# More steps of seven products in a stick-breaking attention trunk, with gated heads spilled as ready halves

## Chip, cores and metric

The kernel runs on one core of one Trainium2 chip. The metric is the device time of one execution, in microseconds (us), and the number given for a kernel is the median of its runs. Engines are named as the profile names them: PE is TensorE (PEld its weight loads), DVE is VectorE, ACT is ScalarE, POOL is GpSimd, SP is SyncE.

## The reference

One layer of attention on x (256 rows of 4096), float32 throughout, and a final norm:

```python
xn = rms_norm(x, norm_attn)                     # (256, 4096)
q, k, v, g = split(xn @ w_in_attn, 4)           # w_in: 4096 x 16384; 32 heads of 128
z = q @ k.T / sqrt(128)                         # per head, 256 x 256
a = sigmoid(z) * prod_{s<j<t}(1 - sigmoid(z_tj))  # s < t, worked out in logs
o = a @ v
h = x + (o * silu(g)) @ w_out_attn              # w_out: 4096 x 4096
out = rms_norm(h, final_norm)
```

The convolution's inputs are not used, since the depth is 1.

## The kernel before

**Splitting.** PE multiplies in a format with a shorter mantissa, so each float32 operand is split in two: ACT copies it into that format (`wh`, `nh`, ...; line 172 for weights), DVE subtracts the copy from the full value (`wl`, `nl`; `minus`, line 98). A product is then three matmuls of 128x128 by 128x512: high by high, high by low, low by high (`mm3`, lines 426 to 428).

**Units and steps.** The work is a list of 21 units (lines 101 to 110). Units 0 to 15 read w_in, two for each of eight column groups j: the even one makes q and k of four heads, the odd one g and v. Units 16 to 20 read w_out: 16 to 18 make two column blocks of 512 each, 19 and 20 one each. A unit runs through 16 steps s; a step takes 256 of the 4096 rows of the weights (two chunks of 128, two column blocks: four pieces of 128x512, 1 MB), and multiplies them with the two row blocks of the activations.

**Seven or eight products.** A step of such 2x2 blocks needs eight products (`EIGHT_PARTS`, or "plain" in units 0, 1 and 16). In the steps named in `SEVEN` it makes seven, from sums of blocks (`SEVEN_PARTS`): three more additions on the weights by DVE (lines 160 to 164), and seven weight pieces to split instead of four. The sums on the activations' side (the "forms") are built once, by `build`, and kept split in SBUF for all units: seven forms for a step in `SEVEN`, six for another, four for a plain one. `combine_early` and `combine_late` put a unit's banks together at its end.

**What sets the order.** Everything is written out in one stream, and the build then orders each engine's instructions, which each engine runs in order. Weight pieces are loaded by SP into three buffers `raw`; the halves of a pair of pieces go into one of `PAIRS` = 4 buffers, a single piece into `SINGLES` = 1; `split` (line 152) is called as far ahead as these allow (lines 690 to 697). A buffer comes free when PE has used it. The remaining work is hung on (unit, step) slots by `at` (lines 571 to 664) and is emitted behind that step's products: for each head `heads_T` (transposes of q and k, and their split), `scores`, `weights_of` (the logs, their suffix sums by matmul, and exponentials), `heads_out`; for each group `gate`, `gate_T`, `v_parts`. `rows_out` (line 379) copies the banks of units 0 and 1.

**Gated heads.** `heads_out` leaves o times the gate in a tile `gated`, which POOL writes to HBM (`spill`, line 497). In unit 15 each step's heads are read back and split (`load_heads`, `build_heads`, what "o"), as w_in's forms of that step are done with; in unit 16 they are read again and built into seven or six forms ("p"), the last two at the end of its step 15; in unit 18 the plain forms of the `SEVEN` steps are built once more ("r"), for the units of one column block.

**Rooms.** Tiles of attention share rooms by tag: `v` (5 buffers: v, its halves, and at the start the loads of x), `f` (2), `qkh`, `qkl` and others (1 each). `gh` (2 buffers) holds what `build` reads and the gated heads.

Of the kernel before, what the change touches and what calls it, by code (L numbers as in the profile page):

```python
# [9 lines left out]
F32 = mybir.dt.float32  # L10
# [27 lines left out]
SEVEN = (2, 4, 6, 9, 11, 13)  # L38
# [11 lines left out]
SEVEN_FORMS = ("A11", "A12", "A22", "S1", "S2", "S3", "S4")  # L50
# [20 lines left out]
def kernel(  # L71
# [41 lines left out]
    for u, (kind, w, cols) in enumerate(units):  # L113
        for s in range(NS):
# [5 lines left out]
            else:  # L120
# [6 lines left out]
                else:  # L127
                    which = SEVEN_PARTS if s in SEVEN else EIGHT_PARTS
# [48 lines left out]
    nc.scalar.dma_start(gcol, gain_in)  # L177
# [4 lines left out]
    def load_x(i):  # L182
        if i >= NS:
            return
        xs[i] = ap.tile([P, KT, S], F32, tag="v", name=f"xs{i}", bufs=5)
        for part in ([slice(0, 1), slice(1, 2)] if i == 0 else [slice(0, 2)]):
            nc.sync.dma_start(xs[i][:, part, :], xT[i][:, part, :])
# [25 lines left out]
    def build(i, y, kind, what):  # L213

        names = {"plain": PLAIN_FORMS, "mixed": SEVEN_FORMS if i in SEVEN else EIGHT_FORMS}[kind]
        h, l = new_forms(i, names, what)

# [3 lines left out]

        if names is not SEVEN_FORMS:
            both(slice(0, 4), y)
            if names is EIGHT_FORMS:
                d = room(f"d{what}{i}", 2)
                y4 = y.rearrange("p (a b) c -> p a b c", a=KT)
                nc.vector.tensor_tensor(out=d, in0=y4[:, :, 0, :], in1=y4[:, :, 1, :], op=ALU.subtract)  # L227
                both(slice(4, 6), d)
            return
        d = room(f"d{what}{i}", 4)  # L230
        tt = nc.vector.tensor_tensor
        tt(out=d[:, 0, :], in0=y[:, 1, :], in1=y[:, 3, :], op=ALU.subtract)
        tt(out=d[:, 1, :], in0=d[:, 0, :], in1=y[:, 0, :], op=ALU.subtract)
        tt(out=d[:, 2, :], in0=y[:, 0, :], in1=y[:, 1, :], op=ALU.subtract)
        tt(out=d[:, 3, :], in0=y[:, 2, :], in1=d[:, 1, :], op=ALU.add)
        both(slice(0, 1), y[:, 0:1, :])
        both(slice(1, 3), y[:, 2:4, :])
        both(slice(3, 7), d)

    def room(name, n):  # L240
        pool, tag = (ap, "f") if ep is None else (ep, "junk")
        return pool.tile([P, n, P], F32, tag=tag, name=name, bufs=2 if ep is None else 1)

    def load_y(src, name):
        y = wp.tile([P, 4, P], F32, tag="gh", name=name, bufs=2)
# [5 lines left out]
    def load_xn(i):  # L251
        if i < NS:
            ys[i] = load_y(xT[i], f"xn{i}")
# [494 lines left out]
```

## Time and profile before

| | |
|---|---|
| median of 3 runs | 1807.13 us (1803.22 to 1808.31) |
| the profiled execution | 1806.54 us; span from first to last instruction 1804.6 us |
| granted TensorE clock, mean | 0.996 |
| ACT busy in the pair of units 12 and 13 (177.1 us) | 108.6 us |
| DMA share and rate in that pair | 0.55, 194 GB/s |
| DMA issues of POOL | 16 of xn, 16 of spill, 16 of o, 16 of p, 6 of r, 256 KB each |

The profile is of one execution. A row of a group gives the line, engine and operation, the tile written and those read, the count, then busy us, mean ns of one, and the idle time of its engine just ahead with what ended it. A row of the timeline begins with the start in us and the duration. A row of a stretch gives its ends and length, then busy us and count of PE, PEld, DVE, ACT and POOL, the granted clock, the DMA engines' share and GB/s. A row of the waits gives who waited, for whom, us in total, times, and the longest.

### The profile page before, as it was taken

To read this page: it belongs to the slowest core of one execution; us is meant where nothing else is said; L and a number is where in the kernel's file an instruction comes from. 1 tells how busy PE (TensorE), PEld (TensorE's weight loads), DVE (VectorE), ACT (ScalarE), POOL (GpSimd) and SP (SyncE) were. 2 spreads that over 40 slices of the span, in tenths; PEclk is the share of its full clock that TensorE was granted. 3 is DMA by queue.
4 is the path that set the end of the run, shared out by engine and by line. 5 is a ranking of instruction groups with operands and counts; after the bars stand their busy time and mean duration, and the time that the engine had idled before them with its cause. 6 is when DMAs were issued, how large, how long until landed. Compare 5 with 4: busy or idle time off the path is not lost. (4 is left out here: it accounts for less than half of the span.)

```text
span 1804.6 us, 22433 instructions
## 1 busy us (share of the span) xinstructions
PE 1778.2 (99%) x8107; PEld 1469.9 (81%) x8107; DVE 1495.3 (83%) x1810; ACT 1089.5 (60%) x1449; POOL 39.5 (2%) x80
## 2 busy tenths in 40 slices
PE   8999999999999999999999999999999999999997
PEld 6888788888888888888888888888887888788885
DVE  5678988888888888888888888888888977889854
ACT  5765665666566656665666565656565756655642
POOL 0000000000000000000000000000001011000000
PEclk9999999999999999999999999999999999999999
DMA  8856555555555545555555555555556666656664
GB/s 313 304 197 223 197 182 195 190 193 197 188 205 191 195 177 216 192 194 184 196 202 186 196 196 193 187 192 190 195 194 221 241 231 219 236 220 239 245 228 150
DMA packets 108814, 374.25 MB, mean 207 GB/s; under 512 B 12704, under 2 KB 12960, under 8 KB 108704
## 3 DMA queue, kind: packets, MB, share of 16 engines
q1 hardware_dynamic: 102960, 354.46, 54.8%
q0 software_dynamic: 5600, 18.35, 3.1%
q8 instruction: 63, 1.03, 0.2%
q14 instruction: 47, 0.39, 0.1%
q10 hardware_dynamic: 144, 0.02, 0.0%
HBM read 364.40 MB, written 8.39 MB: 207 GB/s over the span
## 5 line engine op out<-in xcount | busy, mean ns | idle before, releaser
L172 ACT CAST wh<-raw 128x1024 fp32r<-128x1024 f32 (+1 forms) x833 | 818.8, 1001 | 609.7 <-PE acc L428 274.8
L98 DVE TENSOR_TENSOR wl<-raw,wh 128x1024 fp32r<-128x1024 f32 (+1 forms) x833 | 950.6, 1159 | 245.0 <-ACT wh L172 236.5
L426 PE MATMUL acc<-wh,nh 128*128 128x512 f32 x1708 | 672.9, 394 | 2.2 <-ACT v_sb L383 1.9
L427 PE MATMUL acc<-wl,nh 128*128 128x512 f32 x1708 | 666.4, 390 | 2.7 <-DVE wl L98 2.3
L428 PE MATMUL acc<-wh,nl 128*128 128x512 f32 x1708 | 666.3, 390 | 0.0
L427 PEld LDWEIGHTS acc<-wl,nh 128*128 128x128 f32 x1708 | 321.1, 188 | 68.7 <-DVE wl L98 5.6
L428 PEld LDWEIGHTS acc<-wh,nl 128*128 128x128 f32 x1708 | 320.6, 188 | 68.0
L426 PEld LDWEIGHTS acc<-wh,nh 128*128 128x128 f32 x1708 | 320.9, 188 | 66.4 <-ACT v_sb L383 2.3
L426 PE MATMUL acc<-wh,ph 128*128 128x512 f32 x324 | 125.8, 390 | 2.1 <-ACT wh L172 1.5
L427 PE MATMUL acc<-wl,ph 128*128 128x512 f32 x324 | 126.5, 391 | 0.1
L428 PE MATMUL acc<-wh,pl 128*128 128x512 f32 x324 | 126.1, 389 | 0.0
L160 DVE TENSOR_TENSOR raw<-raw 128x1024 f32<-128x1024 f32 x96 | 117.4, 1223 | 2.3
L426 PE MATMUL acc<-wh,sh 128*128 128x512 f32 x256 | 101.3, 396 | 4.4 <-DVE sh L205 4.4
L427 PE MATMUL acc<-wl,sh 128*128 128x512 f32 x256 | 100.9, 394 | 0.7 <-DVE wl L98 0.6
L428 PE MATMUL acc<-wh,sl 128*128 128x512 f32 x256 | 100.4, 393 | 0.0
L426 PEld LDWEIGHTS acc<-wh,ph 128*128 128x128 f32 x324 | 60.7, 188 | 16.2 <-ACT wh L172 2.7
L427 PEld LDWEIGHTS acc<-wl,ph 128*128 128x128 f32 x324 | 60.8, 188 | 14.0 <-DVE wl L98 1.4
L428 PEld LDWEIGHTS acc<-wh,pl 128*128 128x128 f32 x324 | 60.8, 188 | 12.6
L164 DVE TENSOR_TENSOR raw<-raw 128x512 f32<-128x512 f32 x96 | 66.2, 690 | 2.4
L163 DVE TENSOR_TENSOR raw<-raw 128x512 f32<-128x512 f32 x96 | 66.1, 688 | 1.7
L426 PEld LDWEIGHTS acc<-wh,sh 128*128 128x128 f32 x256 | 48.7, 190 | 15.0 <-ACT wh L172 5.1
L427 PEld LDWEIGHTS acc<-wl,sh 128*128 128x128 f32 x256 | 48.8, 191 | 11.5 <-DVE wl L98 1.5
(167 smaller groups left out, 1374.1 us busy)
## 6 DMA issues: line engine op xcount, KB each, us to landing
raw<-in_w_in_dram SPq DMA_DIRECT2D x510, 512.0 KB, 4.2
raw<-in_w_out_dram SPq DMA_DIRECT2D x128, 512.0 KB, 4.2
xn<-in_xT_dram POOLq DMA_DIRECT2D x16, 256.0 KB, 3.0
xr<-in_x_dram SPq DMA_DIRECT2D x16, 256.0 KB, 5.0
spill<-gated POOLq DMA_DIRECT2D x16, 256.0 KB, 4.1
o<-spill POOLq DMA_DIRECT2D x16, 256.0 KB, 3.6
p<-spill POOLq DMA_DIRECT2D x16, 256.0 KB, 3.8
xres<-in_x_dram SPq DMA_DIRECT2D x16, 256.0 KB, 4.3
```

The lines of the kernel that those rows point to most:

```text
L98: nc.vector.tensor_tensor(out=out_, in0=full, in1=part.bitcast(F32), op=ALU.subtract)
L160: nc.vector.tensor_tensor(out=r[:, 0:3:2, :], in0=r[:, 0:4:3, :], in1=r[:, 2:3, :].broadcast_to([P, 2, CW]), op=ALU.add)
L163: nc.vector.tensor_tensor(out=r[:, 3, :], in0=r[:, 0, :], in1=r[:, 3, :], op=ALU.add)
L164: nc.vector.tensor_tensor(out=r[:, 1, :], in0=r[:, 3, :], in1=r[:, 1, :], op=ALU.add)
L172: nc.scalar.copy(wh[n][:, c, :], f)
L426: nc.tensor.matmul(out_, ah, bh, start=start, stop=False, **kw)
L427: nc.tensor.matmul(out_, ah, bl, start=False, stop=False, **kw)
L428: nc.tensor.matmul(out_, al, bh, start=False, stop=stop, **kw)
```

## The change

- `SEVEN` has eight steps instead of six, for the units of w_in; `SEVEN_OUT` (seven steps) is used for those of w_out. Two steps of seven now stand next to each other in places.
- `build` has no plain kind any more, and puts the sums into the tile that it reads; `room` is gone.
- Gated heads are split once, when they are made (`heads_parts`), and three tiles are spilled: full, high half, low half. The plain forms "o" and "r" are then loaded as halves (`load_parts`), with no work on ACT and DVE. "p" is still built from the full tile; step 15's is built from the tile in SBUF, and the builds of steps 14 and 15 stand in steps 0 and 1 of unit 17.
- v has moved from room `v` (now 4 buffers) to `qkh` and `qkl`, as has the scratch of `gate`; `bound` is one copy of 128x128 that is broadcast; the squares' scratch uses `qkl`.
- Slots of `heads_T`, `scores`, `weights_of`, `heads_out` have moved; `v_parts` stands ahead of `gate`.
- The first piece of x and the gain are issued by ACT instead of SP, ahead of the weights; `rows_out` copies bank C22 ahead of C12.

```diff
-SEVEN = (2, 4, 6, 9, 11, 13)
+SEVEN = (2, 3, 5, 7, 8, 10, 12, 13)
+SEVEN_OUT = (2, 3, 5, 7, 10, 12, 13)
...
-                    which = SEVEN_PARTS if s in SEVEN else EIGHT_PARTS
+                    which = SEVEN_PARTS if s in (SEVEN if w is w_in else SEVEN_OUT) else EIGHT_PARTS
...
-    nc.scalar.dma_start(gcol, gain_in)
...
-        xs[i] = ap.tile([P, KT, S], F32, tag="v", name=f"xs{i}", bufs=5)
-        for part in ([slice(0, 1), slice(1, 2)] if i == 0 else [slice(0, 2)]):
-            nc.sync.dma_start(xs[i][:, part, :], xT[i][:, part, :])
+        xs[i] = ap.tile([P, KT, S], F32, tag="v", name=f"xs{i}", bufs=4)
+        if i:
+            nc.sync.dma_start(xs[i], xT[i])
+            return
+        for k in range(KT):
+            nc.scalar.dma_start(xs[i][:, k, :], xT[i][:, k, :])
+            if k == 0:
+                nc.scalar.dma_start(gcol, gain_in)
...
+        tt(out=y[:, 3, :], in0=y[:, 1, :], in1=y[:, 3, :], op=ALU.subtract)
+        tt(out=y[:, 1, :], in0=y[:, 0, :], in1=y[:, 1, :], op=ALU.subtract)
+        tt(out=y[:, 0, :], in0=y[:, 3, :], in1=y[:, 0, :], op=ALU.subtract)
+        tt(out=y[:, 2, :], in0=y[:, 2, :], in1=y[:, 0, :], op=ALU.add)
+        both(slice(3, 7), y)
...
-    for i in range(RAW_BUFS - 1):
-        load(i)
-        load_x(i)
+    load_x(0)
+    load(0)
+    load_x(1)
+    load(1)
     load_x(2)
...
-        st["v", j] = [ap.tile([P, CW], F32, tag="v", name=f"v_sb{j}_{t}", bufs=5) for t in range(NT)]
+        st["v", j] = [ap.tile([P, CW], F32, tag="qk" + "hl"[t], name=f"v_sb{j}_{t}") for t in range(NT)]
...
+        for dst, r, col, t in ((one, r1, 1, 0), (one, r1, 1, 1), (two, r2, 2, 1), (two, r2, 2, 0)):
+            nc.scalar.activation(dst[t], bank[PLAIN[f"C{t + 1}{col}"]], AF.Copy, scale=r[:, t : t + 1])
...
-        if k == KT - 1:
-            spill[s] = dp.tile([P, 4 * P], F32, name=f"spill{s}")
-            nc.gpsimd.dma_start(spill[s], st["o", s].rearrange("p a b -> p (a b)"))
...
+    def heads_parts(s):
+
+        gated = st["o", s]
+        oh = ap.tile([P, 4, P], F32R, tag="qkh", name=f"oh{s}")
+        ol = ap.tile([P, 4, P], F32R, tag="qkl", name=f"ol{s}")
+        nc.scalar.copy(oh, gated)
+        minus(ol, gated, oh)
+        for what, t in (("f", gated), ("h", oh), ("l", ol)):
+            spill[s, what] = dp.tile([P, 4, P], t.dtype, name=f"spill_{what}{s}")
+            nc.gpsimd.dma_start(spill[s, what], t)
+
+    def load_parts(s, what):
+
+        for part, t in zip("hl", new_forms(s, PLAIN_FORMS, what)):
+            nc.gpsimd.dma_start(t, spill[s, part])
...
-        for i, s in ((0, 2), (1, 8)):
+        for i, s in ((0, 5), (1, 10)):
             at(u + 1, s, heads_T, j, i)
             at(u + 1, s + 1, scores, j, i)
             at(u + 1, s + 3, weights_of, j, i)
+        at(u + 2, 0, v_parts, j)
         at(u + 2, 0, gate, j)
-        at(u + 2, 0, v_parts, j)
...
+            ((3, gate_T, j, 0), (4, heads_out, j, 0), (4, heads_out, j, 1), (4, heads_parts, 2 * j), (7, heads_T, j, 2),
+             (8, scores, j, 2), (10, weights_of, j, 2), (11, gate_T, j, 1), (12, heads_out, j, 2), (12, heads_T, j, 3),
+             (13, scores, j, 3), (15, weights_of, j, 3), (17, heads_out, j, 3), (17, heads_parts, 2 * j + 1))
...
+    for s in range(NS):
+        at(*{NS - 2: (U, 4), NS - 1: (U, 13)}.get(s, (U - 1, max(s, 2))), load_parts, s, "o")
+
+    for s in range(NS - 1):
+        for i in ((0, 1) if s == 0 else (s + 1,)):
+            if i < NS - 1:
+                at(U, s, load_heads, i)
+        at(U + s // (NS - 2), s % (NS - 2), build_heads, s)
+    at(U + 1, 1, lambda: build(NS - 1, st["o", NS - 1], SEVEN_OUT, "p"))
...
+    for s in SEVEN_OUT:
+        at(LAST - 2, s, load_parts, s, "r")
```

More of the change, by code (lines that the diff above doesn't have):

```diff
@@ L278 @@
     make_identity(nc, ident)
-    bound = ap.tile([P, 2, P], F32, name="bound")
+    bound = ap.tile([P, 1, P], F32, name="bound")
     nc.gpsimd.memset(bound, 3e38)
@@ L626 @@
     at(U, 15, make_room)
-    for s in (NS - 2, NS - 1):
-        at(U, 15, build_heads, s, "mixed", "p")
     for c in (0, 1):
```

93 lines of the change are left out of this document (28 added, 65 removed).

## The prediction

> **What bounds the kernel now.** I read the page's busy row first, then the waits of PE, then busy time by stretch, and last the timelines of two places. Units are numbered as the kernel's list has them (0 to 15 read w_in, 16 to 20 w_out); I cut the stretches at a unit's first product, found by counting products in PE's timeline. "Step" is one of a unit's sixteen.
>
> ```profile
> span 1804.6 us, 22433 instructions
> PE 1778.2 (99%) x8107; PEld 1469.9 (81%) x8107; DVE 1495.3 (83%) x1810; ACT 1089.5 (60%) x1449; POOL 39.5 (2%) x80
> ...
> PE acc L426 <- DVE sh L205: 4.4, 1, 4.4
> PE acc L427 <- DVE wl L98: 2.9, 3, 1.4
> PE acc L426 <- ACT v_sb L383: 1.9, 1, 1.9
> PE acc L426 <- ACT wh L172: 1.5, 2, 1.3
> ```
>
> TensorE sets the end: its four longest kinds of wait for others sum to 10.7 us in the whole run, and 4.4 of that is the start. A busy PE isn't yet a PE at its pace, so the pace comes from starts. Here is one step of seven products (unit 12, step 2) and the first product behind it:
>
> ```profile
> 1091.67 0.39 PE L426 MATMUL acc<-wh,nh 128*128 128x512 f32 x1
> ...
> 1096.43 0.39 PE L426 MATMUL acc<-wh,nh 128*128 128x512 f32 x1
> ```
>
> 21 matmuls in 4.76 us: 0.227 us each, though a row says 0.39. A step of eight is 24 of them, 5.45 us.
>
> The stretches are units 12, 13, 15, 17 and 18, then 12 and 13 as a pair:
>
> ```profile
> 1080.80:1170.40 89.60, 89.60 (x421) 74.74 (x420) 78.06 (x90) 55.02 (x71) 0.54 (x1) 1.00 0.53 192
> 1170.40:1257.90 87.50, 87.50 (x404) 72.83 (x403) 74.55 (x84) 53.57 (x68) 0.54 (x1) 1.00 0.56 196
> 1347.60:1438.90 91.30, 89.62 (x403) 72.11 (x401) 82.85 (x99) 59.70 (x83) 8.59 (x16) 1.00 0.63 227
> ...
> 1535.00:1622.10 87.10, 84.85 (x368) 68.26 (x367) 74.47 (x82) 51.29 (x64) 0.00 (x0) 1.00 0.63 226
> 1622.10:1705.30 83.20, 83.20 (x368) 68.60 (x367) 75.84 (x85) 49.74 (x62) 3.22 (x6) 1.00 0.67 240
> ...
> 1080.80:1257.90 177.10, 177.10 (x822) 147.57 (x821) 152.61 (x173) 108.59 (x138) 1.08 (x2) 1.00 0.55 194
> ```
>
> Three things to see. In the pair PE has no gap, and VectorE is busy 152.6 of 177.1 us: near, but behind. Unit 15 has unit 13's products and takes 3.8 us longer. Unit 17 has unit 18's and takes 3.9 longer.
>
> **Products removed.** The fourteen mixed w_in units (2 to 15) go from six to eight steps of seven, the two of w_out (17, 18) from six to seven: 14 x 2 + 2 = 30 steps, three matmuls less in each. 90 x 0.227 = **-20.4 us**, 2.7 in each pair of w_in units. The built order agrees: 8017 matmuls for 8107. All of it lies on the engine that sets the end.
>
> **What a step of seven costs VectorE.** These rows are groups by shape, then a stretch of its timeline:
>
> ```profile
> L98 DVE TENSOR_TENSOR wl<-raw,wh 128x1024 fp32r<-128x1024 f32 x735 | 891.4, 1223 | 238.3 <-ACT wh L172 230.0
> L172 ACT CAST wh<-raw 128x1024 fp32r<-128x1024 f32 x735 | 767.6, 1052 | 582.5 <-PE acc L428 274.8 <-DVE raw L160 204.7 <-DVE raw L164 58.3
> ...
> L98 DVE TENSOR_TENSOR wl<-raw,wh 128x512 fp32r<-128x512 f32 x98 | 67.2, 685 | 6.7 <-ACT wh L172 6.5
> L164 DVE TENSOR_TENSOR raw<-raw 128x512 f32<-128x512 f32 x96 | 66.2, 690 | 2.4
> ```
>
> ```profile
> 1082.75 1.22 DVE L98 TENSOR_TENSOR wl<-raw,wh 128x1024 fp32r<-128x1024 f32 x1
> 1083.88 1.29 DVE L394 SCALAR_TENSOR_TENSOR gl<-g_sb,gl 128x512 f32<-128x512 f32 x2
> ...
> 1089.17 0.69 DVE L98 TENSOR_TENSOR vl<-v_sb,vh 128x512 fp32r<-128x512 f32 x1
> 1089.77 0.69 DVE L163 TENSOR_TENSOR raw<-raw 128x512 f32<-128x512 f32 x1
> ...
> 1091.58 0.68 DVE L164 TENSOR_TENSOR raw<-raw 128x512 f32<-128x512 f32 x1
> 1093.43 5.23 DVE L98 TENSOR_TENSOR wl<-raw,wh 128x1024 fp32r<-128x1024 f32 x5 [1.18 <-ACT wh L172]
> 1098.59 1.22 DVE L160 TENSOR_TENSOR raw<-raw 128x1024 f32<-128x1024 f32 x1
> 1099.84 0.69 DVE L163 TENSOR_TENSOR raw<-raw 128x512 f32<-128x512 f32 x1
> ```
>
> A wide instruction lasts 1.22 us but the next, independent one starts 1.13 to 1.14 later; a narrow one 0.60. One that reads the result starts 1.25 later (1098.59 to 1099.84), 0.11 to 0.12 more, which makes 0.72 for a narrow one. A step of eight is two wide splits, 2.28. A step of seven is three wide splits, a narrow one and three additions: 3.42 + 0.60 + 1.25 + 0.72 + 0.61 = 6.6. Four more such steps in a pair add 4 x 4.3 = 17.3, and the split of the gated heads, new there, 2 x 0.60. So 152.6 + 18.5 = 171.1, while PE's pair shrinks to 174.4. On average VectorE still fits, at 98%, and ScalarE easily does. What decides is where the steps stand.
>
> **The new neighbours.** The sets had no two steps of seven in a row; now 2-3, 7-8 and 12-13 are, so 14 x 3 = 42 places in w_in and 2 x 2 = 4 in w_out. The four pair buffers hold the halves ahead of PE. When PE starts the first seven (time 0), the second's first cast can only begin, as PE has just left the step before. From ScalarE's timeline, the lag behind PE and behind an addition:
>
> ```profile
> 1078.32 1.05 ACT L172 CAST wh<-raw 128x1024 fp32r<-128x1024 f32 x1 [0.24 <-PE acc L428]
> ...
> 1092.35 4.43 ACT L172 CAST wh<-raw 128x1024 fp32r<-128x1024 f32 x5 [1.95 <-DVE raw L164]
> ```
>
> The second seven then goes: cast 0.24 to 1.3; on VectorE the first split to 2.4, L160 to 3.6, the narrow split to 4.2, L163 to 4.8, a wide split to 5.9, L164 until 6.6; only then the last cast, 0.1 + 1.05, to 7.8; the last split ends at 9.0 (L160 and L163 are taken at their shorter spacing, as the built order puts other work between). PE wants it at 4.76 + 15 x 0.227 + 0.23 = 8.4. So a place is 0.6 us short before any attention work. A lone seven, as before, has a step of eight ahead of it, in which VectorE needs 2.3 us and PE 5.45, and comes in time. The built order of the changed kernel puts two matmuls that need only the cast in front of that wait (-0.2), and in some places the next step's or the attention's products. Attention work on VectorE between the two makes it worse: the gate in 2-3, scores and splits in 7-8 and 12-13. I followed both orders of one pair of units through with these spacings. The even unit is short by 0.25 at step 3, 1.45 at step 8 (split of the gated heads and gating stand ahead), 0 at 13; the odd one by 0.25, 0.55 and 0.5. That is 3.0 in six places, **0.5 each; 46 x 0.5 = +23.0 us**. Ends: 0 (before's sevens, lone, cost PE nothing in the pair's row) and 1.2 (no reordered product helps, and one more narrow instruction, 0.60, stands in each). I take 0.5, between, since it follows the order that is built.
>
> **The start.** PE's first product waited for VectorE's L205, that for the transfer of xs:
>
> ```profile
> 9.47 0.76 PE L426 MATMUL acc<-wh,sh 128*128 128x512 f32 x1 [4.35 <-DVE sh L205]
> ...
> 4.19 1.50 DVE L98 TENSOR_TENSOR wl<-raw,wh 128x512 fp32r<-128x512 f32 x2 [2.99 <-ACT wh L172]
> 8.97 0.35 DVE L205 TENSOR_SCALAR sh<-xs,gcol 128x256 fp32r<-128x256 f32 x1 [3.28 <-DMA xs<-in_xT_dram]
> ...
> 2.66 0.91 SPq L187 DMA_DIRECT2D xs<-in_xT_dram  x2
> ```
>
> SP issued those after four weight loads, at 2.66; now ScalarE's queue issues them first, at about 0.8. The two splits before L205 end at 5.7, so the most to be had is 3.3. **-3.0**; nothing if the transfers, now beside the same weights, land no earlier.
>
> In these rows the early products start 0.43 apart (not 0.227):
>
> ```profile
> 10.46 0.63 PE L426 MATMUL acc<-wh,sh 128*128 128x512 f32 x1
> 10.88 0.63 PE L428 MATMUL acc<-wh,sl 128*128 128x512 f32 x1
> ```
>
> The Trainium skill, "TensorE: Matmul & The Clock Gate", "What's actually happening", says the array's clock is halved after an idle window of about 3.4 us. By that rule a start whose gap behind the warm-up shrinks from 4.4 to about 1 would keep the full clock and save some 2 us more, an estimate from that page and eleven such products; no row here shows it, and the sum leaves it out.
>
> **Other parts.** Unit 15 loses the sixteen loads and splits of the heads (ready halves are loaded instead): back to unit 13's time, **-3.8** (nothing, if its additions are the cause). Two builds leave step 15 of unit 16 for steps 0 and 1 of unit 17, behind the bank copies: of unit 17's 3.9 I take **-2.9** (0 to 3.9). The order of L383's copies frees the waited bank one copy earlier: **-0.6** of the 1.9. Two more seven-forms to split in unit 1: **+0.5** (0 to 2). POOL issues 55 more DMAs, far apart and under PE's work, except the last heads' write and read before step 15 of unit 16: 0 to +2.5; I take 0, as six products of unit 17 stand ahead there in the built order. The moved rooms and the shared `bound` add waits on work long done: 0.
>
> Sum: 1806.5 (the profiled execution; its span is 1804.6, and the median of the three runs 0.6 more) - 20.4 - 3.0 - 3.8 - 2.9 - 0.6 + 23.0 + 0.5 = **1799.3**, call it 1799.
>
> **The rivals.**
> - *The last split of the second seven is later than I think.* Every wait of an in-order queue there (cast behind a single's buffer, gating behind PE) adds to the chain above. Of the gains 30.7, minus 0.5, is used up at 0.66 us a place; at 1.0 the time is 1822. For it: 98% of VectorE, and the 1.18 us that it already waits at 1093.43 for that same cast. Against: PE's reordered products.
> - *The buffers cover it.* At 0.15 a place: 1783. For it: in the pair's row, PE waited for none of twelve sevens.
> - *VectorE's instructions stop overlapping when it is full.* 88 wide instructions in the pair start 0.09 early, 8 us; with full durations it needs 160.5, and 4 x (6.95 - 2.45) + 1.4 more: 179.9 for 177.1. 7 x 2.8 = 20 later instead of the 19.1 less of the w_in products: 1806.5 + 20 - 11.1 = 1815. Against: the spacings above. The Trainium skill, "VectorE: DVE Perf Modes", "The DRAIN you can't avoid", says that the next instruction does not start until the pipe has emptied; the 1.13 us behind a 1.22 us instruction speaks against it here.
> - *It doesn't do what it says at the seams*: units 15 and 17 keep their waits, as loads now come late instead of splits: 1806.
>
> **How the numbers follow.** Forecast (0.3 to 0.65 a place, 1790 to 1806): 0.42. Late split: 0.25. Cover: 0.23. No overlap: 0.05. Seams: 0.05. About 0.3% of the median, 5.4 us, is what a measurement of this kernel can tell from no change: faster is below 1801.7, slower above 1812.6. Faster: cover 0.23 and 0.30 of the forecast, 0.53. Slower: 0.24 of late split, 0.05 of no overlap, 0.29. Same: the remaining 0.18. Range 1783 to 1820: it reaches the cover's time and most of the late split.
>
> **What would show it.** 8017 products; PE's first one near 6.5; pairs of w_in units at 176 to 179 us with VectorE near 97% busy; PE waiting some 20 us in all for wl, in many waits of under 1.5 us, at steps 3, 8 and 13 and hardly elsewhere; units 15 and 17 no longer than 13 and 18. If PE's waits for wl sum to under 8 us, the buffers cover; over 31, the change loses. It would be wrong altogether if waits appear at lone sevens, or behind the spill.

## The result, and the profile after

| kernel | median | runs | ratio to before (95% interval) |
|---|---|---|---|
| before | 1805.99 us | 1803.22 to 1808.31 (4) | |
| after | 1820.09 us | 1818.83 to 1822.56 (4) | 1.0080 (1.0061 to 1.0099) |

The change made the kernel slower by 0.8%, some 14 us. The forecast was 1799, and its range ended at 1820, 0.09 under the time measured. The profiled execution took 1822.56 us, 16.0 more than the profiled one of before.

The page of the changed kernel, its span and its row of busy engines:

```profile
span 1820.8 us, 22601 instructions
...
PE 1780.9 (98%) x8017; PEld 1451.9 (80%) x8017; DVE 1601.8 (88%) x1966; ACT 1128.2 (62%) x1506; POOL 68.5 (4%) x135
```

The 90 matmuls are gone (8107 to 8017), as counted, and yet the span has grown by 16.2 us: PE makes fewer products, but is busy 2.7 us longer (1778.2 before) and idle 13.5 us longer. Its waits of most weight (who waited, for whom, us, times, the longest):

```profile
PE z L418 <- DVE qkl L99: 7.4, 3, 4.8
PE acc L418 <- DMA oh<-spill_h: 4.4, 1, 4.4
PE acc L418 <- ACT wh L173: 4.3, 10, 1.2
...
PE acc L419 <- DVE wl L99: 1.7, 3, 0.8
```

The two at the top are new, few and long: single places, not a rate. To find them, cut the run at the units' first products, found by counting products. These are units 1 and 16 of before, which the prediction did not show:

```profile
99.50:191.60 92.10, 91.41 (x414) 75.16 (x413) 74.70 (x136) 54.40 (x86) 7.51 (x14) 1.00 0.64 214
1438.90:1535.00 96.10, 95.28 (x445) 78.70 (x444) 74.14 (x125) 58.96 (x94) 9.66 (x18) 1.00 0.62 223
```

And of after: units 1, 15 and 16, then 12 and 13 as a pair:

```profile
96.90:197.70 100.80, 93.66 (x413) 77.22 (x412) 77.95 (x145) 55.41 (x89) 7.51 (x14) 0.97 0.56 197
...
1356.80:1445.90 89.10, 87.96 (x397) 71.23 (x396) 81.94 (x95) 54.57 (x70) 17.00 (x32) 1.00 0.83 280
1445.90:1550.80 104.90, 98.72 (x446) 79.71 (x445) 76.64 (x130) 61.61 (x99) 12.41 (x23) 0.97 0.67 227
...
1089.20:1267.00 177.80, 177.13 (x810) 144.79 (x810) 167.93 (x195) 115.51 (x148) 3.21 (x6) 1.00 0.56 199
```

Units 1 and 16 are longer by 8.7 us each, more together than the whole run. The pair is 0.7 longer though it lost 2.7 of products. Units 15 and 17 are shorter, by 2.2 and 1.6; unit 18 is 2.1 longer (the lengths of 17 and 18 are in the table of the experiments).

**Unit 1.** VectorE's timeline ahead of the longest wait, then ScalarE's:

```profile
134.80 0.29 DVE L99 TENSOR_TENSOR nl<-xn,nh 128x128 fp32r<-128x128 f32 x1
137.03 0.48 DVE L253 SCALAR_TENSOR_TENSOR xn<-xn,gcol,rows 128x256 f32<-128x256 f32 x1 [1.94 <-DMA xn<-in_xT_dram]
...
138.36 1.22 DVE L99 TENSOR_TENSOR wl<-raw,wh 128x1024 fp32r<-128x1024 f32 x1
139.50 0.28 DVE L237 TENSOR_TENSOR xn<-xn 128x128 f32<-128x128 f32 x1
139.70 0.68 DVE L99 TENSOR_TENSOR qkl<-tr,qkh 128x512 fp32r<-128x512 f32 x1
```

```profile
135.05 0.58 ACT L410 CAST qkh<-tr 128x512 fp32r<-128x512 f32 x1
...
140.94 1.14 ACT L225 CAST nh<-xn 128x512 fp32r<-128x512 f32 x2 [4.37 <-DVE xn L239]
```

The high half `qkh` was there at 135.63, but VectorE subtracted it only at 139.70: the queue ahead waited 1.94 us for a load of xn and then did multiplications, splits and the first two additions of a build in their turn. ScalarE in turn stood 4.37 us for the last of that build's additions. Over the whole unit (window 97 to 198) these two waits are:

```profile
ACT nh L225 <- DVE xn L239: 20.7, 6, 4.9
DVE xn L253 <- DMA xn<-in_xT_dram: 17.5, 12, 3.3
```

With another addition of the builds (L231: 6.5 us) ScalarE waits 27.2 us for additions. Before, it was 4.9 us, and VectorE's wait for xn 11.9 us in 13. PE came in only at 140.44:

```profile
140.44 0.47 PE L418 MATMUL z<-qkh 128*128 128x128 f32 x1 [4.81 <-DVE qkl L99]
...
141.89 0.63 PE L418 MATMUL acc<-wh,sh 128*128 128x512 f32 x1
142.31 0.63 PE L419 MATMUL acc<-wl,sh 128*128 128x512 f32 x1
...
145.73 0.43 PE L418 MATMUL acc<-wh,sh 128*128 128x512 f32 x1
```

Behind the gap nine products start 0.43 apart, not 0.227: 1.8 us more. So this place costs about 6.6, and a second wait for `qkl`, of 2.33 us at 174.52 (shown at the end), most of the rest.

**Unit 16.** How the last heads came back before the change (step 15's products need them):

```profile
1523.44 0.42 DVE L494 TENSOR_TENSOR gated<-o,gT 128x256 f32<-128x256 f32 x1 [1.05 <-PE o L428]
...
1524.16 0.55 POOL L497 DMA_DIRECT2D spill<-gated  x1 [9.64 <-DVE gated L494]
...
1527.03 0.54 POOL L502 DMA_DIRECT2D o<-spill  x1 [2.32 <-DMA spill<-gated]
...
1530.58 0.62 ACT L219 CAST oh<-o 128x512 fp32r<-128x512 f32 x1 [0.51 <-DMA o<-spill]
...
1531.25 0.50 PE L426 MATMUL acc<-wh,oh 128*128 128x512 f32 x1 [0.50 <-ACT oh L219]
```

And after it:

```profile
1534.30 0.42 DVE L486 TENSOR_TENSOR gated<-o,gT 128x256 f32<-128x256 f32 x1
...
1535.85 0.54 POOL L497 DMA_DIRECT2D spill_h<-oh  x1 [0.30 <-ACT oh L493]
...
1537.35 0.54 POOL L497 DMA_DIRECT2D spill_l<-ol  x1
1541.05 0.54 POOL L502 DMA_DIRECT2D oh<-spill_h  x1 [3.17 <-DMA spill_h<-oh]
...
1543.59 0.53 POOL L502 DMA_DIRECT2D ol<-spill_l  x1 [1.99 <-DMA spill_l<-ol]
```

From the gate to the first cast it took 7.1 us (1523.44 to 1530.58), and 7.8 to PE's first product with these heads, with the full tile alone. Now the chain is gate, split, write, read: the low half's write is issued at 1537.35, its read at 1543.59. PE's own rows show when both came:

```profile
1544.10 0.80 PE L418 MATMUL acc<-wh,oh 128*128 128x512 f32 x1 [4.42 <-DMA oh<-spill_h]
...
1548.18 0.94 PE L420 MATMUL acc<-wh,ol 128*128 128x512 f32 x2 [0.29 <-DMA ol<-spill_l]
```

That is 9.8 us behind the gate for the high half and 13.9 for the low one, and the gate itself comes 3.9 us later in its unit than before (88.4 for 84.5 us). So the first product with these heads stands 5.8 us later in its unit; 3.9 of that is the late gate, and 2.0 the longer chain. Why the gate is late no run isolates.

### The profile page after: what moved, and what is told of

It reads as the page before. It is cut to its first block, busy times and chain, and to the rows that moved or that the text cites. A ratio compares the mean times of both kernels' runs of the same rounds, so it can differ in the third digit from the quotient of the medians.

```text
span 1820.8 us, 22601 instructions
## 1 busy us (share of the span) xinstructions
PE 1780.9 (98%) x8017; PEld 1451.9 (80%) x8017; DVE 1601.8 (88%) x1966; ACT 1128.2 (62%) x1506; POOL 68.5 (4%) x135
## 5 line engine op out<-in xcount | busy, mean ns | idle before, releaser
L173 ACT CAST wh<-raw 128x1024 fp32r<-128x1024 f32 (+1 forms) x893 | 856.6, 988 | 550.2 <-DVE raw L161 228.9
L99 DVE TENSOR_TENSOR wl<-raw,wh 128x1024 fp32r<-128x1024 f32 (+1 forms) x893 | 995.3, 1144 | 150.8 <-ACT wh L173 143.8
L419 PE MATMUL acc<-wl,nh 128*128 128x512 f32 x1680 | 659.6, 393 | 1.9 <-DVE wl L99 1.3
L418 PE MATMUL acc<-wh,nh 128*128 128x512 f32 x1680 | 654.1, 396 | 2.7 <-ACT wh L173 1.7
L420 PE MATMUL acc<-wh,nl 128*128 128x512 f32 x1680 | 656.0, 390 | 0.0
L419 PEld LDWEIGHTS acc<-wl,nh 128*128 128x128 f32 x1680 | 315.9, 188 | 72.9 <-DVE wl L99 9.4
L418 PEld LDWEIGHTS acc<-wh,nh 128*128 128x128 f32 x1680 | 314.1, 188 | 73.6 <-ACT wh L173 12.3
L161 DVE TENSOR_TENSOR raw<-raw 128x1024 f32<-128x1024 f32 x126 | 153.8, 1221 | 1.4
L418 PE MATMUL acc<-wh,sh 128*128 128x512 f32 x256 | 101.7, 397 | 1.3 <-DVE sh L210 1.3
L165 DVE TENSOR_TENSOR raw<-raw 128x512 f32<-128x512 f32 x126 | 86.9, 690 | 2.8
L164 DVE TENSOR_TENSOR raw<-raw 128x512 f32<-128x512 f32 x126 | 87.0, 690 | 2.7
L420 PEld LDWEIGHTS acc<-wh,pl 128*128 128x128 f32 x314 | 59.0, 188 | 11.9
L420 PEld LDWEIGHTS acc<-wh,sl 128*128 128x128 f32 x256 | 48.9, 191 | 11.8 <-DVE sl L213 1.4
```

Source lines behind the costliest of these rows:

```text
L99: nc.vector.tensor_tensor(out=out_, in0=full, in1=part.bitcast(F32), op=ALU.subtract)
L161: nc.vector.tensor_tensor(out=r[:, 0:3:2, :], in0=r[:, 0:4:3, :], in1=r[:, 2:3, :].broadcast_to([P, 2, CW]), op=ALU.add)
L164: nc.vector.tensor_tensor(out=r[:, 3, :], in0=r[:, 0, :], in1=r[:, 3, :], op=ALU.add)
L165: nc.vector.tensor_tensor(out=r[:, 1, :], in0=r[:, 3, :], in1=r[:, 1, :], op=ALU.add)
L173: nc.scalar.copy(wh[n][:, c, :], f)
L418: nc.tensor.matmul(out_, ah, bh, start=start, stop=False, **kw)
```

## The experiments

Unit lengths in us, cut at first products in each profiled execution ("even/odd": the medians of the steady units 4 to 13); the ratio is that to before, with its 95% interval.

| run | 1 | 2 | even/odd | 16 | 17 | 18 | median | ratio |
|---|---|---|---|---|---|---|---|---|
| before | 92.1 | 93.5 | 89.7/87.4 | 96.1 | 87.0 | 83.2 | 1805.99 | |
| after | 100.8 | 92.7 | 89.8/87.9 | 104.8 | 85.4 | 85.3 | 1820.09 | 1.0080 (1.0061 to 1.0099) |
| e1_direct | 102.6 | 91.3 | 89.8/87.9 | 98.1 | 90.0 | 84.6 | 1820.07 | 1.0078 (1.0063 to 1.0093) |
| e2_room | 102.8 | 91.5 | 89.8/87.9 | 104.9 | 85.6 | 84.6 | 1823.67 | 1.0096 (1.0081 to 1.0112) |
| e3_slots | 99.5 | 94.7 | 89.8/87.9 | 105.4 | 85.5 | 85.3 | 1824.39 | 1.0098 (1.0082 to 1.0113) |
| e4_oldsets | 101.7 | 94.8 | 90.0/87.4 | 106.1 | 83.0 | 83.0 | 1817.63 | 1.0068 (1.0051 to 1.0085) |
| e5_sums | 92.5 | 94.8 | 89.8/87.9 | 105.5 | 85.4 | 85.0 | 1816.08 | 1.0055 (1.0035 to 1.0075) |
| e6_sums_slots | 90.7 | 95.2 | 89.8/87.9 | 105.5 | 85.5 | 84.6 | 1815.53 | 1.0052 (1.0037 to 1.0068) |
| e7_apart | 102.1 | 92.2 | 93.0/87.2 | 105.2 | 83.3 | 82.3 | 1836.18 | 1.0161 (1.0142 to 1.0180) |
| e8_seams | 90.7 | 95.3 | 89.8/87.9 | 98.4 | 90.4 | 84.7 | 1812.79 | 1.0032 (1.0022 to 1.0043) |
| g1_seven_apart | 90.7 | 94.1 | 90.5/86.7 | 102.3 | 88.6 | 82.6 | 1804.74 | 0.9995 (0.9984 to 1.0006) |
| g2_eight_one | 95.0 | 92.7 | 90.7/87.5 | 102.1 | 86.3 | 82.3 | 1813.37 | 1.0040 (1.0027 to 1.0054) |
| g3_sums_all | 90.7 | 94.0 | 90.5/86.7 | 95.7 | 82.3 | 82.6 | 1792.41 | 0.9923 (0.9911 to 0.9936) |
| g4_seven_one | 90.7 | 93.8 | 90.1/87.1 | 95.7 | 86.9 | 84.4 | 1800.03 | 0.9968 (0.9957 to 0.9979) |
| h1_sums_own | 90.7 | 92.5 | 89.8/87.9 | 108.1 | 84.9 | 84.6 | 1815.43 | 1.0057 (1.0042 to 1.0072) |
| h2_sums_direct | 91.2 | 93.2 | 89.8/87.9 | 96.4 | 89.7 | 84.6 | 1809.11 | 1.0021 (1.0011 to 1.0030) |
| h3_no_direct | 91.2 | 94.3 | 90.5/86.7 | 106.2 | 82.8 | 82.6 | 1804.24 | 0.9991 (0.9980 to 1.0002) |
| h4_v_late | 90.7 | 93.3 | 89.4/86.7 | 96.0 | 82.3 | 82.9 | 1785.51 | 0.9890 (0.9876 to 0.9905) |
| i1_pair23 | 90.7 | 92.7 | 89.7/87.1 | 95.7 | 86.0 | 84.2 | 1795.67 | 0.9944 (0.9929 to 0.9959) |
| i2_pair78 | 90.7 | 91.9 | 89.8/87.6 | 95.7 | 83.8 | 83.3 | 1795.57 | 0.9944 (0.9927 to 0.9961) |

### First round: one suspect each

**e1_direct**, the round trip of step 15's heads.

```diff
+        if s == NS - 1:
+            h, l = new_forms(s, PLAIN_FORMS, "o")
+            nc.scalar.copy(h, gated)
+            minus(l, gated, h)
+            return
```

> The heads of step 15 are split straight into the stationary tiles of unit 16 (both halves written where the products read them), so their two writes to DRAM and two reads back are gone; nothing else changes. Theory (unit 16 is 8.7 us longer because its last step waits for that round trip, a gap of 4.8 us, 0.9 more, and some ten products at half pace behind it): unit 16 goes from 104.8 to 97 or 98 us, the total to 1812 to 1814, and PE's wait of 4.4 us for oh from spill_h is gone. Rival (the denser list of the last heads fills VectorE and PE waits anyway): PE waits for the split of the heads instead, unit 16 stays at 103 or more, the total at 1818 or more.

Units 16 and 17 of this run:

```profile
1443.70:1541.80 98.10, 95.96 (x445) 78.62 (x444) 72.70 (x122) 58.99 (x95) 9.17 (x17) 1.00 0.63 218
1541.80:1631.90 90.10, 84.89 (x365) 67.47 (x364) 81.83 (x95) 54.78 (x71) 0.54 (x1) 1.00 0.60 220
```

Unit 16 did what the theory said, 6.7 us shorter at full clock. But unit 17 took 4.6 back, and the median did not move: PE now waits there for casts, bank copies and splits (`wh`, `h`, `wl`). It may be that these had caught up during the gap; no run isolates that. A wait taken away shows the next one.

**e2_room**, more room for the loads of xn.

```diff
-            ys[i] = wp.tile([P, 4, P], F32, tag="gh", name=f"xn{i}", bufs=2)
+            ys[i] = ap.tile([P, 4, P], F32, tag="v", name=f"xn{i}", bufs=4)
```

> In unit 1 the loads of xn get four buffers of the attention pool that lie idle then, in place of the two that the builds now hold until their last split; the builds still add in place, and slots and sets stay. Theory (unit 1 is 8.7 us longer because the additions in place hold the buffer, so that the next load is issued late, and VectorE's queue stands behind it with the split that PE waits for): VectorE's waits for xn (17.5 us in 12) go to under 4, PE's waits for qkl (7.4 us in 3) to under 1.5, unit 1 from 100.8 to 92.5 to 94 us, the total to 1811 to 1814. Rival 1 (the first heads' slots, moved from steps 2 and 8 to 5 and 10, put the split behind builds): unit 1 stays at 99 or more. Rival 2 (two builds of seven in a row fill VectorE): unit 1 ends between 96 and 99, without waits for xn.

The theory falls: unit 1 takes 102.8 us. VectorE's wait in that run:

```profile
DVE xn L253 <- DMA xn<-in_xT_dram: 18.3, 11, 3.3
```

It was 17.5 us in 12. With four buffers the built order only put the multiplications further ahead, so that each again stood right behind its load. More buffers alone are no remedy. As the wait did not go, the run doesn't show that late loads have no part in it.

**e3_slots**, the first heads' transposes where they were.

```diff
-        for i, s in ((0, 5), (1, 10)):
+        for i, s in ((0, 2), (1, 8)) if j == 0 else ((0, 5), (1, 10)):
```

> Only in unit 1 the heads' transposes go back to steps 2 and 8, as before; the buffers of xn stay two and held to the end of the build. Theory (late loads of xn hold VectorE's queue wherever the transposes stand): unit 1 stays at 97 us or more, VectorE waits for xn 14 us or more. Rival (the moved slots are the cause): unit 1 comes to 92.5 to 94.5 us and PE's waits for qkl vanish.

Unit 1 at 99.5 us: 1.3 less, and unit 2 is 2.0 longer. The slots are not the cause of the 8.7.

**e4_oldsets**, the sets of before.

```diff
-SEVEN = (2, 3, 5, 7, 8, 10, 12, 13)
-SEVEN_OUT = (2, 3, 5, 7, 10, 12, 13)
+SEVEN = (2, 4, 6, 9, 11, 13)
+SEVEN_OUT = (2, 4, 6, 9, 11, 13)
```

> The changed kernel with the sets of before (2, 4, 6, 9, 11, 13 in both), so six steps of seven and no neighbours; all else as changed. Theory (a pair of w_in units lost 2.7 us of products and took on 3.3 of stalls at the neighbours): pairs come back to 177.0 to 177.4 us from 177.7, so the sets are worth some -4 us over the seven pairs, and units 1 and 16 stay long (98 or more, 103 or more) as their causes are elsewhere: total 1812 to 1818. Rival (the heads' one split and its three writes load the pairs, not the neighbours): pairs grow to 179 or more, as the removed products come back and the stalls stay; total 1828 or more.

As the theory had it: a pair of 177.4 us, units 1 and 16 still long (101.7, 106.1). So neither is a matter of the sets: even with none of the new steps of seven, the rest of the change costs 0.7%.

### Second round: the additions in place

**e5_sums** and **e6_sums_slots** (with e3's slots as well): in unit 1 the sums get tiles of their own and come ahead of the casts.

```diff
+            d = ap.tile([P, n, P], F32, tag="v", name=f"d{i}", bufs=4)
...
+            tt(out=d[:, 3, :], in0=y[:, 1, :], in1=y[:, 3, :], op=ALU.subtract)
+            tt(out=d[:, 1, :], in0=y[:, 0, :], in1=y[:, 1, :], op=ALU.subtract)
+            tt(out=d[:, 0, :], in0=d[:, 3, :], in1=y[:, 0, :], op=ALU.subtract)
+            tt(out=d[:, 2, :], in0=y[:, 2, :], in1=d[:, 0, :], op=ALU.add)
+            both(slice(0, 1), y[:, 0:1, :])
+            both(slice(1, 3), y[:, 2:4, :])
+            both(slice(3, 7), d)
```

> Unit 1's builds put their sums in tiles of their own again (in room that unit 1 leaves idle), ahead of the casts as before the change, so that no addition waits for a cast of the same tile and the buffer of xn comes free one split earlier; builds of the heads still add in place; slots, sets and spills as changed. Theory now (more buffers alone did nothing, so it is the chain split, additions, cast, split in place that puts waits into the queues of ScalarE, 27 us for the additions, and VectorE): unit 1 falls from 100.8 to 92.5 to 95 us, ScalarE's wait for the additions under 8 us, total 1812 to 1815. Rival (the moved slots, or the rooms that the heads now share with other work): unit 1 stays at 98 or more.

> As the run with sums in tiles of their own, and the first heads' transposes of unit 1 back at steps 2 and 8. Theory: no more than 1 us from the slots, unit 1 at 92 to 95 us. Rival (both are needed): unit 1 is 3 us or more shorter than with the sums alone.

Unit 1 of e6_sums_slots:

```profile
96.30:187.00 90.70, 90.70 (x414) 75.43 (x413) 75.57 (x143) 55.28 (x88) 7.53 (x14) 1.00 0.62 217
```

That settles where unit 1's time went: 8.3 us come back with the sums alone, 1.8 more with the slots (between what theory and rival had for them), and then PE has no gap in it. In the same window of e5_sums ScalarE's longest kind of wait for an addition and VectorE's for xn are:

```profile
DVE xn L270 <- DMA xn<-in_xT_dram: 12.0, 12, 2.6
...
ACT nh L225 <- DVE d L240: 2.5, 4, 1.3
```

The wait for additions is gone (27.2 to 2.5), and that for xn is back at the 11.9 us that it was before the change. Not all of the gain arrives: in the profiled executions unit 2 grows by 2.1 and 2.5, unit 15 by 1.7 and 0.5, and the medians gain 4.0 and 4.6. An addition that writes over a value must wait until ScalarE has cast it and VectorE has subtracted the cast; a build that was additions, casts, splits became cast, split, additions, cast, split, and each crossing holds up the rest of two in-order queues.

**e7_apart**, steps of seven without neighbours: sets (0, 2, 4, 6, 8, 10, 12, 14) and (0, 2, 4, 6, 8, 10, 12).

> The changed kernel with eight steps of seven in w_in that have no neighbours (0, 2, 4, 6, 8, 10, 12, 14) and seven in w_out (0, 2, 4, 6, 8, 10, 12). Theory (the neighbours are what costs 3.3 us a pair, not VectorE's load as such): a pair falls from 177.7 to 174.4 to 175.2 us, the total to 1796 to 1804. Rival (VectorE at 98% of PE's time cannot follow wherever the steps stand): the pair stays at 177 us or more, the total at 1816 or more. What may blur it: step 14 now delays the early combination of the banks into step 15.

The theory was wrong; the rival has the numbers (a pair of 180.2, 1836 in all), but not the reason, as it isn't even. Odd units are 0.7 shorter than in the change, units 17 and 18 2.1 and 3.0; only the even ones are 3.2 longer, and PE's waits tell where:

```profile
PE trg L397 <- DVE g_sb L390: 7.5, 6, 1.4
```

The gate is late: the late combination of the gate's banks (L353) starts 1.1 us into unit 12, in the change 3.0 us ahead of it. That fits what was feared beside the expectation, step 14 holding up `combine_early`. This run did not isolate the neighbours.

**e8_seams**: e6_sums_slots and e1_direct together.

> Both seams mended in one: sums of unit 1 in their own tiles, its slots as before, and the heads of step 15 split straight into the stationary tiles, with the sets of the change. Theory: unit 1 at 92 to 95, unit 16 at 97 to 98.5, unit 17 at 90 (what the round trip hid comes out there), total 1807 to 1811: with the neighbours' 3.3 a pair that is no faster than before. Rival (the waits only move on): 1815 or more.

1812.79, between the two: units 16 and 17 (98.4, 90.4) as the theory had them, unit 1 shorter (90.7), but unit 2 (95.3) keeps some of it. All seams mended, the sets of the change still lose to before by 0.3%.

### Third round: where the steps stand (all on e8_seams)

**g1_seven_apart**: (1, 3, 5, 7, 9, 11, 13) in both sets. **g4_seven_one**: (2, 3, 5, 7, 9, 11, 13). **g2_eight_one**: (0, 2, 4, 6, 8, 10, 12, 13) and (0, 2, 4, 6, 8, 10, 12).

> Both seams mended, and seven steps of seven without neighbours (1, 3, 5, 7, 9, 11, 13) in w_in and in w_out. The run with eight apart also moved steps 0 and 14; this one leaves both as steps of eight. Theory (neighbours cost PE 3.3 us a pair; apart, a step of seven is free, as before the change): a pair is 177.1 less two steps' products, 1.4: 175.7 to 176.2 us; units 17 and 18 lose 2 to 4 us each, since each had two neighbours; total 1795 to 1801. Rival (each further step of seven costs VectorE's time wherever it stands): a pair of 177 us or more, total 1807 or more.

> As the run with seven apart, with the sets (2, 3, 5, 7, 9, 11, 13): as many steps of seven, but one neighbour pair in each unit. Theory (a neighbour costs about 0.5 us in w_in): a pair is 0.7 to 1.4 us longer than with seven apart, units 17 and 18 some 1 us each, total 6 to 11 us more. Rival (neighbours are free, the number of steps of seven decides): the same pair within 0.3 us.

> As that run, with eight steps in w_in: 0, 2, 4, 6, 8, 10, 12, 13, one neighbour pair and step 14 left alone; w_out has 0, 2, 4, 6, 8, 10, 12. Theory (the 93 us of even units in the run with eight apart came from step 14, which holds up the early combination of the banks and the gate behind it): even units under 89 us, a pair of 175 to 176. Rival (step 0 is the place that hurts, where the gate already fills both queues): even units 90.5 us or more, a pair of 178 or more.

Of g1_seven_apart an even unit, an odd one and unit 18:

```profile
544.20:634.70 90.50, 89.88 (x419) 73.92 (x417) 83.02 (x96) 57.88 (x75) 1.61 (x3) 1.00 0.55 197
634.70:721.40 86.70, 86.70 (x400) 72.15 (x399) 79.63 (x90) 55.03 (x69) 1.61 (x3) 1.00 0.55 201
1621.10:1703.70 82.60, 82.60 (x364) 68.06 (x363) 76.11 (x83) 47.06 (x56) 7.43 (x14) 1.00 0.77 267
```

One step more than before should take 0.68 us from each. The odd unit lost 0.7 and unit 18 0.6, with no gap on PE: apart, a step of seven is free there, though VectorE is busy 79.6 of 86.7 us. With one neighbour pair (g4_seven_one) the odd unit is 0.4 longer and unit 18 1.8. But g1's even unit is 0.8 longer than before, not 0.7 shorter, and PE waits right behind its step 1 (11.7 us into the unit), where VectorE has the gate and the split of v:

```profile
555.84 0.50 PE L436 MATMUL acc<-wl,nh 128*128 128x512 f32 x1 [0.53 <-DVE wl L99]
```

So g1's pair (177.2) bears out the rival in its number and the theory in its odd half, and its median, 1804.74, lies between the two. g4_seven_one missed: forecast 6 to 11 us above g1, it came out 4.7 below, with the same pair (177.2), as its even unit is 0.4 shorter and its unit 16 takes 95.7 for 102.3. In g1's unit 16 PE waited 4.2 us in one piece for `qkl`, as in unit 1 of the change. g2_eight_one has its rival's numbers (even units 90.7, a pair of 178.2); that step 0 is what hurts isn't isolated, as 12-13 are neighbours in it.

**g3_sums_all**: g1_seven_apart, with tiles of their own for the sums of the heads' builds too (steps 14 and 15 excepted), in the scores' room `f`.

> As the run with seven apart, and the builds of the heads for w_out get sums in tiles of their own too, in the room that seven forms less leave free (steps 14 and 15 excepted, whose builds fall behind the closing of that room). Theory (adding in place made chains between the queues in unit 16 as in unit 1): unit 16 from some 98 to 95 to 97 us, total 1 to 3 us less than the run with seven apart. Rival (unit 16's rest comes from the heads' denser list): unit 16 within 0.7 us, total the same.

1792.41, faster than before by 0.8% (0.64 to 0.89%), and 12.3 us under g1_seven_apart where 1 to 3 were expected: unit 16 fell from 102.3 to 95.7 and unit 17 from 88.6 to 82.3. Neither alone does that for unit 17: with the sums apart but neighbours (h2_sums_direct, below) it stays at 89.7.

### Fourth round: what was open

**h1_sums_own** puts the sums apart at the change's own sets (three slots in `f`, the fourth sum over a value that is not cast; one cast and split more). **h2_sums_direct** adds e1_direct. **h3_no_direct** is g3_sums_all with the round trip back.

> The changed kernel with its own sets, slots and spills; only the builds differ: every sum that would overwrite a value still to be cast goes to a tile of its own (room idle in unit 1, the scores' tile in unit 16), at the price of one narrow cast and split more in a build of seven; the builds of steps 14 and 15 for w_out stay in place. Theory (additions in place tie the queues together in unit 16 as in unit 1, and only then does the round trip of the last heads show): unit 1 92 to 94, unit 16 from 104.8 to 97 to 99.5, units 16 and 17 together 6 us or more shorter, total 1806 to 1811. Rival (the round trip has its price by itself): unit 16 at 103 or more, total 1813 or more.

> As that, and the heads of step 15 split straight into the stationary tiles. Theory: little is left for it, less than 2 us against the run with the sums alone, total 1804 to 1810. Rival (the round trip has its own price): 4 us or more less than with the sums alone.

> The fastest kernel so far (seven steps of seven apart, all sums in tiles of their own, slots of unit 1 as before) with the round trip of the heads of step 15 put back. Theory (hidden once the queues run freely): unit 16 up by less than 1.5 us, total 1792 to 1795. Rival (a write and a read of 6.0 and 4.5 us behind the last heads cannot be hidden in step 13 to 15): units 16 and 17 up by 4 to 7 us, total 1796 to 1800.

Unit 16 in the first two:

```profile
1438.60:1546.60 108.00, 99.60 (x445) 79.79 (x444) 77.02 (x140) 64.05 (x108) 12.38 (x23) 0.95 0.67 225
```

```profile
1435.70:1532.10 96.40, 95.53 (x445) 78.65 (x445) 73.65 (x135) 61.45 (x104) 9.69 (x18) 1.00 0.63 218
```

The theory falls and the rival holds in both; in h3_no_direct the price is more than even its rival had (11.0 us for 4 to 7, and 1804.24 in all). The round trip has its own price: without it units 16 and 17 together are 6.9 us shorter at the change's sets (193.0 to 186.1; medians 6.3 apart), and with it 11.0 longer at the seven apart (178.0 to 189.0). The sums in place are little of the 8.7 at the change's sets: with the round trip left in, taking them apart brings nothing (h1's unit 16 is even longer than after's, with PE's clock halved for 10.2 us of it instead of 6.8), and with it gone 1.7 us (98.1 in e1_direct to 96.4).

**h4_v_late**: g3_sums_all, with the split of v two steps later, and the gate's scratch in `f`, so that the gate doesn't wait for v.

```diff
-        at(u + 2, 0, v_parts, j)
         at(u + 2, 0, gate, j)
+        at(u + 2, 2, v_parts, j)
...
-            l = ap.tile([P, CW], F32, tag="qk" + "hl"[t], name=f"gl{j}_{t}")
+            l = ap.tile([P, CW], F32, tag="f", name=f"gl{j}_{t}", bufs=2)
```

> The fastest kernel so far, with the split of v moved from step 0 of the even units to step 2 (the gate's scratch back in the scores' tile, so that the gate does not wait for v). Theory (what is left of a pair's loss stands at step 1 of the even unit, where VectorE has the gate and the split of v beside a step of seven): even units from 90.5 to 89.0 to 89.8 us, pairs 175.7 to 176.5, total 1782 to 1788. Rival (the gate alone fills the place, or the split only moves the wait to step 3): even units at 90.2 or more, total 1790 or more.

An even unit:

```profile
541.40:630.80 89.40, 89.16 (x418) 74.06 (x417) 82.65 (x96) 56.57 (x73) 1.61 (x3) 1.00 0.56 200
```

The theory holds: even units 1.1 shorter, the pair 176.1, the median 1785.51, 1.1% (0.95 to 1.24%) faster than before. How much each of the two moves gives is not shown. This is the best version found.

**i1_pair23** and **i2_pair78**: h4_v_late with one neighbour pair in each mixed unit, at 2-3, then at 7-8.

> The fastest kernel (sums and heads as there, split of v late), with the sets (2, 3, 5, 7, 9, 11, 13): one neighbour pair, 2 and 3, in each mixed unit. Theory (by the prediction's count, 0.25 us a place in w_in, and some 1.8 in units 17 and 18 as in the run with one neighbour pair before): odd units 87.0 to 87.2 us, even ones 89.5 to 90.0, unit 18 84.4, total 1789 to 1794. Rival (free, once the rest is out of the way): pairs within 0.2 us of 176.1, total 1784 to 1787.

> The same with the sets (1, 3, 5, 7, 8, 11, 13): the neighbours are 7 and 8. Theory (by the prediction's count, 1.45 us in an even unit, where the split of the gated heads and the gating stand ahead, 0.55 in an odd one): even units 90.5 to 91, odd ones 87.1 to 87.4, total 1797 to 1801. Rival (the products pulled ahead cover it): pairs within 0.5 us of 176.1.

The price of one neighbour pair: at 2-3 0.4 us in an odd unit and 0.3 in an even one, at 7-8 0.9 and 0.4; in unit 18 1.3 and 0.4, in unit 17 3.7 and 1.5. Both medians are 10 us above h4_v_late, for one neighbour pair a unit and the same number of matmuls. (One step moves in each, 1 to 2 and 9 to 8, and the price is that of the move as a whole.) The theory of i1_pair23 has the units right, its total is 1.7 us over; that of i2_pair78 has the even unit too long (90.5 to 91) and the odd one a little short (87.1 to 87.4), and its rival (pairs within 0.5 us) fails too, at 177.4.

## Why the prediction was wrong

Its sum was -7.2 us on the profiled execution; it measured +16.0. Of the 23.2 between, units 1 and 16 hold 16.9.

- **Products removed, -20.4:** right (8017; 0.227 apart).
- **Unit 1, "+0.5 (0 to 2)": this step failed.** It priced the builds by their instructions, "two more seven-forms to split", and "the moved rooms ... add waits on work long done: 0". It measured +8.7, and e5_sums shows why: the additions in place. The order of a build was in the diff; what it does to two in-order queues, one of which also waits 12 us in 13 pieces for xn, was never followed through. As each built instruction was there to follow, it should have been. Late loads of xn stand in the same chain, and no run parts the two.
- **The round trip of the last heads, "0 to +2.5; I take 0, as six products of unit 17 stand ahead there": the second failure.** Unit 16 measured +8.7, and 6.7 of that goes with the round trip in e1_direct. The six matmuls of unit 17 that run ahead of the gap cover 1.4 us. Before's own rows, had they been laid end to end, show 7.1 us from the gate to the cast; the change put the split ahead of the write and set three writes into POOL's queue where there was one. The bound of 2.5 had no such sum behind it. The gate, 3.9 us later in its unit, was not in the sum either. What taking the round trip away is worth at the median depends on what stands behind it: 0 (e1_direct), 6.3 (h1_sums_own to h2_sums_direct), 11.8 (h3_no_direct to g3_sums_all).
- **The new neighbours, 46 x 0.5 = +23.0:** right in size. Units 3 to 14 took 1062.5 us before and 1066.3 after; with 24 x 0.68 = 16.3 of products gone, the stalls are 20.1 us in 36 places, 0.56 each. (Of these, 0.3 a pair is no neighbour's: e4_oldsets has it too. That leaves 0.51.) The 0.25 at step 3 is 0.3 to 0.4. At step 8 the two halves were the wrong way about: 0.4 in the even unit (1.45 forecast), 0.9 in the odd one (0.55). At step 13 the even unit was to lose nothing, and there (unit 12) its products are furthest behind their pace, by 0.7 us. And w_out, with 4 places at 0.5, paid more: unit 18 is 2.7 us shorter with seven apart, 1.35 a place.
- **How it would show** was wrong. PE's waits for `wl` and `wh` sum to only 6 us, which by the prediction's mark ("under 8 us, the buffers cover") would have meant 1783. The stall shows instead in the starts. In the pair of units 12 and 13 the products start 3.4 us later in sum than at 0.227 each, for 1.4 before; 2.1 of the 3.4 stand in steps 3, 8 and 13, as the prediction had the places. The 88 intervals behind attention's matmuls take 1.4 us more than before (10.9 for 9.5). The view of waits lists little of either; the stretches cut by unit show it.
- **VectorE near 97%:** 167.9 of 177.8 us, 94%. The rival of no overlap is out: at 138.36 a 1.22 us subtraction is followed at 139.50 by the next instruction, 1.14 later, and in the pair 65 of 80 wide splits are followed 1.13 to 1.14 us later. The Trainium skill ("VectorE: DVE Perf Modes", "The DRAIN you can't avoid") has the next operation wait for the pipe to empty, but ends with the exception that one that is not held starts earlier. The prediction left the exception out; these rows agree with it.
- **The start, -3.0:** right, 9.47 to 6.63.
- **The copies of L383, -0.6:** not borne out. PE's wait for `v_sb`, 1.9 us before, is absent in the changed kernel, but it is 2.1 us in e6_sums_slots, with the same order of copies and unit 1 without a gap.
- **Unit 15, -3.8:** with its two steps and three places, -3.7 was forecast for the unit; it measured -2.2. **Unit 17, -2.9:** with one step and two places -2.6; it measured -1.6. Some 40% short. Unit 17's gain is in part luck: where the gap ahead of it goes at the same sets (e1_direct), it takes 90.0 us, 3.0 more than before.
- **The rivals.** The late split forecast 1822 and the time is 1820, which is luck: a place costs 0.56, not 1.0, and the rest came from units 1 and 16. "It doesn't do what it says at the seams" had the right place and the wrong seams: 15 and 17 gained, 1 and 16 lost.

Left open: why unit 17 is 90 us rather than 85 whenever the round trip goes at the change's sets (e1_direct, e8_seams, h2_sums_direct). Neighbours at 2-3 cost it 3.7 in i1_pair23, which fits, but its builds of steps 14 and 15 were not moved in any run. Open too is why unit 2 grows when unit 1 shrinks (92.7 to 95.2 in e6_sums_slots, with PE's wait for `v_sb` back and a half clock behind it, but 95.3 in e8_seams without the half clock).

## What to carry to other kernels

When a change makes a tile's sums overwrite their own inputs, or puts a split ahead of a transfer, write out the new chain engine by engine, in order, with durations from the rows, and compare its length with the time until PE needs the end; pricing by added instructions misses it. A step that is free alone is not free beside its like: measure places, not totals. And an experiment that removes a wait without moving the time (e1_direct) has not refuted it: look at the next stretch.

## What the runs showed of the hardware

- TensorE's clock. PE's rows at the start and at unit 1's second wait:

```profile
6.63 0.47 PE L418 MATMUL acc<-wh,sh 128*128 128x512 f32 x1 [1.35 <-DVE sh L210]
6.94 0.40 PE L419 MATMUL acc<-wl,sh 128*128 128x512 f32 x1
...
9.37 0.63 PE L418 MATMUL acc<-wh,sh 128*128 128x512 f32 x1
...
12.36 0.54 PE L419 MATMUL acc<-wl,sh 128*128 128x512 f32 x1
```

```profile
174.52 0.33 PE L418 MATMUL z<-qkh 128*128 128x128 f32 x1 [2.33 <-DVE qkl L99]
...
175.31 0.40 PE L418 MATMUL acc<-wh,sh 128*128 128x512 f32 x1
```

Behind waits of 4.8 us (unit 1) and 4.4 (unit 16) nine and seven products start 0.43 us apart, behind one of 2.3 none (six attention matmuls in 0.79 us, where they took 1.45 at 140.44); the granted clock reads 0.50 from 141.89 to 145.73 and 0.53 from 1544 to 1549, but 1.00 from 174.5 to 178. So the two long waits cost some 1.8 and 1.4 us more than their length. Length alone does not decide: in e6_sums_slots a wait of only 2.05 us (191.18 to 193.23) was followed by half a clock from 193.51 to 196.92. In the records of the clock such stretches last 3.41 us, or two or three times that (6.83 behind either long wait here, 10.24 in unit 16 of h1_sums_own), and in one execution they start and end on one grid of 3.41 us. Laid on the grid of its own run, the wait of 2.05 lies in one such step, that of 2.33 across two. The Trainium skill ("TensorE: Matmul & The Clock Gate", "What's actually happening") has the clock halved by an idle window of about 3.4 us that runs freely; the grid agrees, though the step ahead of the half clock in e6_sums_slots was not all idle: PE waited through 2.05 of its 3.41 us. What share of a step must be idle no run shows. The 2 us that it might have saved at the start, by the prediction's estimate, did not come: the first products are at full pace (granted clock 0.99 from 6.6 to 9.3), but from 9.37 to 12.36 eight start 0.43 apart all the same (0.51).

- POOL's transfers of 256 KB. In a view of the transfers around the last heads (us to landing at the end):

```profile
spill_f<-gated POOLq DMA_DIRECT2D x1, 256.0 KB, 2.5
spill_h<-oh POOLq DMA_DIRECT2D x1, 256.0 KB, 4.7
spill_l<-ol POOLq DMA_DIRECT2D x1, 256.0 KB, 5.7
```

Three in a row land later and later, and a read for a build (`p` from `spill_f`, 1536.74) stands in the same queue between the second and the third; before, the lone write let its reader go within 2.9 us (1524.16 to 1527.03). Over the whole run a write's median landing went from 4.1 us to 6.0. The Trainium skill ("DMA: Bandwidth & Descriptors", "Anatomy of one DMA — SWDGE (gpsimd) path") gives about 2.0 us plus the bytes over 436 GB/s, 2.6 for these as an estimate from that page; the first agrees, the two behind it do not.
